# Gate projections of three branches by seven products of half size instead of eight

## The chip, the cores and the metric

The kernel runs on one core of a Trainium2 chip. The metric is the device time of one run in microseconds, the median of several. The engines named below are PE (matmuls, with its weight loads), DVE, ACT and POOL (elementwise), and SP, whose queue issues the DMAs.

## The reference

Two layers of a mixer. Each takes 1152 tokens (128 of a prompt, 1024 of a sample) of width 1024, modulates and normalises them to h, and projects h by one matrix w_in to the inputs of three branches and to a merge gate for each:

```
fx, fz, rq, rk, rv, rz, aq, ak, av, az, mg = split_columns(h @ w_in)
ya = (fourier_mix(fx) @ w_four) * silu(fz)
yb = rms_norm(retention(rq, rk, rv)) * silu(rz)
yc = windowed_attention(aq, ak, av) * silu(az)
ga, gb, gc = split(sigmoid(mg), 3)
merged = ga * (ya @ w_pa) + gb * (yb @ w_pb) + gc * (yc @ w_pc)
x = x + gate * rms_norm(merged @ w_out)
```

The gates mg are 3072 columns of w_in: the largest projection of a layer. The change concerns them, and the products with w_pa, w_pb and w_pc that they scale.

## The kernel before

h lies transposed in SBUF, features on the partitions, eight tiles of 128 features by 1152 tokens, split into a high and a low part (HH, HL) of fp32r. A weight tile is split in the same way: ACT casts the high part (L174), POOL subtracts (L175). A product of the two is three matmuls, high by high, high by low, low by high. A gate tile of 128 columns is loaded as one unit of 512 KB, `unit_t`; for each of three chunks of 384 tokens, `proj_t` (L214 to L221) runs 8 x 3 matmuls into a PSUM bank.

The layer runs in stages: the projection of retention's keys and values, constants of retention, the Fourier branch, retention over nine tiles of tokens (`ret_a` makes scores, L817 to L825; `ret_b` the output and its norm, L842 to L866), queries of attention, the gates az of attention, attention itself (nine tiles), and the output projection. `branch(br, ...)` (L904 to L959) computes for a branch: the rows of its y from DRAM; then per 128 output columns the gate tile, its tanh (L938), the branch product (L941 to L943), the scaling of one by the other (L944, DVE), the sum with the branch before (L956, POOL), a store to DRAM. Branches 0 and 1 stand behind attention in the program, branch 2 behind them with its result kept in SBUF.

The framework orders the instructions of each engine ahead of time by a simulated timeline, and every engine then runs its list in order. So the matmuls of branches 0 and 1, which need only h and y, are placed between those of retention's end and of attention. A list is fixed: an engine whose next instruction waits does nothing else. `tick()` (L481) steps the modulation of the next layer (L446, DVE) beside the projections.

The retention's result is stored by SP (L879) after its ninth tile. The DMAs of w_in's gate columns are issued by SP too (L188).

## Time and profile before

| | |
|---|---|
| median of 3 runs | 2015.68 us (2013.76 to 2015.83) |
| profiled execution | 2026.52 us, span 2024.7 us |
| PE | 1968.2 us, 97% |
| DVE | 1033.1 us, 51% |
| ACT | 676.1 us, 33% |
| POOL | 551.5 us, 27% |

The profiled execution is 0.5% slower than the median. The busy time of a matmul overlaps that of the next, so a mean duration on the page is a latency; what a matmul costs PE is the distance between two starts in the timeline. The stages of the first layer that the change touches are, by PE: the end of retention (396 to 455 us), attention (455 to 835), and the gates behind it (835 to 934); in the second layer 1390 to 1441, 1441 to 1792 and 1792 to 1920.

### The profile page before, as it was taken

Reading aid. Unit: us, or ns where it says so; the run is one execution under the profiler, and the core shown is the slowest. Engines: PE = TensorE matmul, PEld = TensorE weight load, DVE = VectorE, ACT = ScalarE, POOL = GpSimd, SP = SyncE. Lnnn points to the kernel's source line nnn. Section 1 sums busy time; section 2 is a strip of 40 time slices with the busy share of each in tenths; the row PEclk is TensorE's granted clock in tenths of the full one; section 3 lists DMA queues with packets and bytes.
Section 4 is the critical chain, followed back from the end, with each engine's and each line's share of the span. In section 5 each row is a group of like instructions: output and inputs, shape, how many; then the busy total and the mean of one; then the engine's idle time right before and its main releaser. Section 6 shows DMA issues by size and latency. Waiting matters only on the chain.

```text
span 2024.7 us, 30761 instructions
## 1 busy us (share of the span) xinstructions
PE 1968.2 (97%) x11334; PEld 1818.2 (90%) x11334; DVE 1033.1 (51%) x2675; ACT 676.1 (33%) x1563; POOL 551.5 (27%) x424
## 2 busy tenths in 40 slices
PE   5999999999999999999999999999999999999998
PEld 2898888999999999999877978799999999999987
DVE  6726556545677775414674262434356655531411
ACT  3522111214444555414331212022345554531411
POOL 2222232121122221254441203122121223234342
PEclk8999999999999999999999999999999999999999
DMA  8323553434343332333344134233333333342142
GB/s 293 100 71 100 155 148 117 129 117 137 112 123 114 114 102 65 116 118 128 118 142 96 58 94 146 82 118 95 124 107 102 108 101 97 93 132 90 55 146 93
DMA packets 245190, 230.58 MB, mean 114 GB/s; under 512 B 37920, under 2 KB 215856, under 8 KB 244784
## 3 DMA queue, kind: packets, MB, share of 16 engines
q1 hardware_dynamic: 245040, 228.62, 37.5%
q8 instruction: 89, 1.46, 0.3%
q14 instruction: 61, 0.50, 0.1%
HBM read 170.14 MB, written 58.42 MB: 113 GB/s over the span
## 4 chain that ended last, share of the span: by engine, by line
PE 88%; DVE 4%; DMA 4%; issue 1%; ACT 1%; SPq 1%; POOL 0%; DVEq 0%; POOLq 0%; ACTq 0%
PE pj L218 13%; PE pj L219 13%; PE pj L220 13%; PE pj L229 5%; PE pj L228 5%; PE pj L230 5%; PE pv L1099 4%; PE tr L1092 3%; PE sl L1038 2%; PE sl L941 2%; PE sl L943 2%; PE sl L942 2%; DMA raw<-in_w_in 2%; PE pj L941 2%; PE pj L942 2%; PE sl L230 2%
## 5 line engine op out<-in xcount | busy, mean ns | idle before, releaser
L218 PE MATMUL pj<-HH,uh 128*128 128x384 f32 x1440 | 496.0, 344 | 11.9 <-DVE XL L653 5.7
L220 PE MATMUL pj<-HH,ul 128*128 128x384 f32 x1440 | 491.5, 341 | 0.0
L219 PE MATMUL pj<-HL,uh 128*128 128x384 f32 x1440 | 489.6, 340 | 0.0
L175 POOL TENSOR_TENSOR ul<-raw,uh 128x1024 fp32r<-128x1024 f32 x80 | 193.6, 2421 | 513.9 <-ACT uh L174 420.4
L218 PEld LDWEIGHTS pj<-HH,uh 128*128 128x128 f32 x1440 | 273.5, 190 | 16.7 <-DVE XL L653 6.0
L219 PEld LDWEIGHTS pj<-HL,uh 128*128 128x128 f32 x1440 | 273.7, 190 | 0.7
L220 PEld LDWEIGHTS pj<-HH,ul 128*128 128x128 f32 x1440 | 273.3, 190 | 1.0
L174 ACT CAST uh<-raw 128x1024 fp32r<-128x1024 f32 x80 | 83.9, 1049 | 176.3 <-PE pj L219 108.2
L446 DVE SCALAR_TENSOR_TENSOR macc<-mw,siluc,macc 128x256 f32<-128x256 f32 x224 | 134.1, 639 | 8.4 <-DMA mw<-in_w_mod 8.4
L228 PE MATMUL pj<-uh,HH 128*128 128x512 f32 x336 | 134.1, 400 | 3.5 <-ACT kv L546 1.9
L229 PE MATMUL pj<-ul,HH 128*128 128x512 f32 x336 | 133.5, 397 | 0.0
L230 PE MATMUL pj<-uh,HL 128*128 128x512 f32 x336 | 132.9, 396 | 0.0
L1075 ACT ACTIVATE E<-E,NM 128x640 f32<-128x640 f32 (+1 forms) x128 | 101.8, 798 | 53.0 <-DVE NM L1071 52.9
L1095 ACT CAST Eh<-tr 128x512 fp32r<-128x512 f32 (+1 forms) x136 | 76.3, 574 | 113.9 <-PE tr L1092 101.0
L1096 DVE TENSOR_TENSOR El<-tr,Eh 128x512 fp32r<-128x512 f32 (+1 forms) x136 | 90.6, 671 | 36.3 <-ACT Eh L1095 29.7
L956 POOL TENSOR_TENSOR mth<-mth,ml 128x384 f32<-128x384 f32 x48 | 52.1, 1086 | 187.6 <-DVE mth L944 144.3
L944 DVE SCALAR_TENSOR_TENSOR M<-M,sl 128x384 f32<-128x384 f32 x48 | 26.5, 553 | 133.1 <-PE sl L943 132.6
L1056 DVE CUSTOM_DVE_ANT_0 E<-sl,mask,m 128x384 f32<-128x384 f32 (+1 forms) x128 | 71.9, 580 | 30.4 <-PE sl L1038 30.0
L1092 PE MATMUL tr<-ident,E 128*128 128x128 f32 x528 | 85.6, 273 | 0.0
L228 PEld LDWEIGHTS pj<-uh,HH 128*128 128x128 f32 x336 | 63.4, 189 | 18.4 <-ACT kv L546 2.1
L1052 DVE TENSOR_SCALAR_CACHE_REDUCE E<-sc 128x256 f32<-128x256 f32 x128 | 49.3, 421 | 60.1 <-PE sc L1038 59.4
L944 DVE SCALAR_TENSOR_TENSOR mth<-mth,pj 128x384 f32<-128x384 f32 x96 | 52.9, 551 | 52.4 <-ACT mth L938 27.8
(305 smaller groups left out, 4134.8 us busy)
## 6 DMA issues: line engine op xcount, KB each, us to landing
raw<-in_w_in SPq DMA_DIRECT2D x84, 512.0 KB, 4.0
scr_m<-mth SPq DMA_DIRECT2D x96, 192.0 KB, 2.4
mw<-in_w_mod SPq DMA_DIRECT2D x128, 128.0 KB, 2.5
scr_n<-ns SPq DMA_DIRECT2D x36, 256.0 KB, 2.4
ml<-scr_m SPq DMA_DIRECT2D x48, 192.0 KB, 2.5
mrow<-scr_m SPq DMA_DIRECT2D x16, 576.0 KB, 5.1
big<-in_w_mod SPq DMA_DIRECT2D x16, 512.0 KB, 4.8
raw<-in_w_out SPq DMA_DIRECT2D x16, 512.0 KB, 4.0
```

Of the source, the lines that this page charges most:

```text
L174: ACT.copy(hi, raw)
L175: POOL.tensor_tensor(out=lo, in0=raw, in1=f(hi), op=ALU.subtract)
L218: PE.matmul(acc, hi[:, k, :], HH[:, k, tok], start=(k == 0), stop=False)
L219: PE.matmul(acc, hi[:, k, :], HL[:, k, tok], start=False, stop=False)
L220: i = PE.matmul(acc, lo[:, k, :], HH[:, k, tok], start=False, stop=(k == KT - 1))
L228: PE.matmul(acc, a, hi[:, k % 2, :], start=(k == 0), stop=False)
L229: PE.matmul(acc, a, lo[:, k % 2, :], start=False, stop=False)
L230: i = PE.matmul(acc, b, hi[:, k % 2, :], start=False, stop=(k == KT - 1))
L446: DVE.scalar_tensor_tensor(out=accs[s], in0=w, scalar=siluc[:, k, s : s + 1], in1=accs[s], op0=ALU.mult, op1=ALU.add,)
L1075: ACT.activation(Es[hh][:, 0:nk], srcs[hh], AF.Exp, bias=NM[t][:, hs + hh : hs + hh + 1], scale=0.125, accum_out=DEN[t][:, hs + hh : hs + ...
L1092: PE.transpose(pt[:, i, hh, :], Es[hh][:, (n + i) * P : (n + i + 1) * P], ident)
L1096: DVE.tensor_tensor(out=El[:, :w], in0=pt, in1=f(Eh[:, :w]), op=ALU.subtract)
```

## The change

A gate pair is two column blocks (256 columns) by half of the tokens (576, in two halves of 288). Halves of the 1024 features, of the pair's columns and of the tokens make a 2 by 2 block product, which Strassen's scheme in Winograd's form computes by seven block products instead of eight. Each block product is 4 k-tiles x 3 matmuls of 288 columns (L953 to L960, `product`); a pair has 84. The sums of weights and of outputs are made in `gate_pair` (L964 to L1016): the weights' by DVE and POOL, on the raw tile, and each operand is then split by ACT and POOL; the outputs' by DVE. The sums of h, T1 to T4, depend on no gate column and are computed once a layer, after the first projection stage (L577 to L598); they and three blocks of h itself that are wanted again later go to DRAM, high and low part. `gates_half(s)` (L1036) loads them into the regions of HH and HL given by the table AT, when h itself is used no more, and runs all three branches for half s. The gates of branch 2 go to DRAM (gc_d); `merge` (L1074) reads them and branch 1's sum per tile of 128 columns. Attention's E buffers go from 6 to 4 and the weight pool wp is closed for the gates' stage.

```diff
 TOK = NT * P
 CH = 384
 NCH = 3
+SC = 576
+HN = 288
...
+        with pool("tp", side="right") as tp:
+            for s in range(2):
+                lt, rt = slice(s * SC, s * SC + HN), slice(s * SC + HN, (s + 1) * SC)
+                k1, k2 = slice(0, 4), slice(4, 8)
+                b = {}
+                for n, ks, tk in (("12", k1, rt), ("11", k1, lt), ("22", k2, rt), ("21", k2, lt)):
+                    b[n] = mk(tp, [P, 4, HN], "b" + n)
+                    POOL.tensor_tensor(out=b[n], in0=f(HH[:, ks, tk]), in1=f(HL[:, ks, tk]), op=ALU.add)
+                    if "B" + n in BLK[s]:
+                        for i, H in enumerate((HH, HL)):
+                            SP.dma_start(blk_dl[l][s]["B" + n][i].rearrange("p (a b) -> p a b", a=4), f(H[:, ks, tk]))
+                DVE.tensor_tensor(out=b["11"], in0=b["12"], in1=b["11"], op=ALU.subtract)
+                DVE.tensor_tensor(out=b["12"], in0=b["22"], in1=b["12"], op=ALU.subtract)
+                DVE.tensor_tensor(out=b["22"], in0=b["22"], in1=b["11"], op=ALU.subtract)
+                DVE.tensor_tensor(out=b["21"], in0=b["21"], in1=b["22"], op=ALU.subtract)
+                for n, t in (("T2", "22"), ("T3", "12"), ("T1", "11"), ("T4", "21")):
+                    th = mk(tp, [P, 4, HN], "th", F32R, bufs=2)
+                    tl = mk(tp, [P, 4, HN], "tl", F32R, bufs=2)
+                    ACT.copy(th, b[t])
+                    DVE.tensor_tensor(out=tl, in0=b[t], in1=f(th), op=ALU.subtract)
+                    for i, x in enumerate((th, tl)):
+                        SP.dma_start(blk_dl[l][s][n][i].rearrange("p (a b) -> p a b", a=4), f(x))
...
+        def block(s, n):
+            k0, t0 = AT[s][n]
+            return HH[:, k0 : k0 + 4, t0 : t0 + HN], HL[:, k0 : k0 + 4, t0 : t0 + HN]
+        def load_block(s, n):
+            for i, x in enumerate(block(s, n)):
+                SP.dma_start(f(x), blk_dl[l][s][n][i].rearrange("p (a b) -> p a b", a=4))
+        def operand(src, eng=POOL):
+            hi, lo = (mk(gp, [P, 4, P], t, F32R, bufs=5) for t in ("oh", "ol"))
+            ACT.copy(hi, src)
+            eng.tensor_tensor(out=lo, in0=src, in1=f(hi), op=ALU.subtract)
+            return hi, lo
+        def product(acc, op, s, n, start, stop):
+            hi, lo = op
+            bh, bl = block(s, n)
+            for k in range(4):
+                PE.matmul(acc, hi[:, k, :], bh[:, k, :], start=start and k == 0, stop=False, skip_group_check=True)
+                PE.matmul(acc, hi[:, k, :], bl[:, k, :], start=False, stop=False, skip_group_check=True)
+                i = PE.matmul(
+                    acc, lo[:, k, :], bh[:, k, :], start=False, stop=stop and k == 3, skip_group_check=True
+                )
+            anchor["pe"] = i.ins
+        def gate_pair(c0, s, eng):
+            w = []
+            for h in range(2):
+                raw = mk(gp, [P, 4, 256], "raw", bufs=2)
+                last_w[0] = SP.dma_start(
+                    raw, w_in[h * 512 : h * 512 + 512, c0 : c0 + 256].rearrange("(k p) f -> p k f", p=P)
+                ).ins
+                w.append(raw)
+            a11, a12, a21, a22 = w[0][:, :, 0:P], w[1][:, :, 0:P], w[0][:, :, P:256], w[1][:, :, P:256]
+            def comb(eng, x, y, op):
+                o = mk(gp, [P, 4, P], "sf", bufs=3)
+                eng.tensor_tensor(out=o, in0=x, in1=y, op=op)
+                return o
+            def add(o, x, y):
+                anchor["dve"] = DVE.tensor_tensor(out=o, in0=x, in1=y, op=ALU.add).ins
+            th = [mk(mA, [P, SC], "gt", bufs=3) for _ in range(2)]
+            lt, rt = slice(0, HN), slice(HN, SC)
+            def tanh(j, tk, src=None):
+                ACT.activation(th[j][:, tk], th[j][:, tk] if src is None else src, AF.Tanh, scale=0.5)
+                tick()
+            o1 = operand(a11, eng)
+            s1 = comb(POOL, a21, a22, ALU.add)
+            s2 = comb(DVE, s1, a11, ALU.subtract)
+            x1 = pj([P, HN])
+            product(x1, o1, s, "B11", True, False)
+            p1 = mk(mA, [P, HN], "p1")
+            ACT.copy(p1, x1)
+            x2 = pj([P, HN])
+            product(x2, operand(s2), s, "T2", True, True)
+            s4 = comb(DVE, a12, s2, ALU.subtract)
+            u2 = mk(mA, [P, HN], "u2", bufs=2)
+            add(u2, p1, x2)
+            product(x1, operand(a12, eng), s, "B21", False, True)
+            tanh(0, lt, x1)
+            x3 = pj([P, HN])
+            product(x3, operand(comb(POOL, a11, a21, ALU.subtract)), s, "T3", True, False)
+            u3 = mk(mA, [P, HN], "u3")
+            add(u3, u2, x3)
+            x4 = pj([P, HN])
+            product(x4, operand(s1), s, "T1", True, False)
+            add(th[1][:, rt], u3, x4)
+            tanh(1, rt)
+            product(x3, operand(a22, eng), s, "T4", False, True)
+            add(th[1][:, lt], u2, x3)
+            tanh(1, lt)
+            product(x4, operand(s4), s, "B22", False, True)
+            add(th[0][:, rt], u2, x4)
+            tanh(0, rt)
+            return th
+        def weights_of(pl, wb, nk, c0, n):
+            braw = mk(pl, [P, nk, n], "braw")
+            SP.dma_start(braw, wb[:, c0 : c0 + n].rearrange("(k p) f -> p k f", p=P))
+            bh = mk(pl, [P, nk, n], "bh", F32R, bufs=2)
+            bl = mk(pl, [P, nk, n], "bl", F32R, bufs=2)
+            ACT.copy(bh, braw)
+            POOL.tensor_tensor(out=bl, in0=braw, in1=f(bh), op=ALU.subtract)
+            return bh, bl
+        def mixed(pb, bh, bl, YH, YL, tok):
+            nk = len(YH)
             for kt in range(nk):
+                PE.matmul(pb, bh[:, kt, :], YH[kt][:, tok], start=(kt == 0), stop=False)
+                PE.matmul(pb, bh[:, kt, :], YL[kt][:, tok], start=False, stop=False)
+                PE.matmul(pb, bl[:, kt, :], YH[kt][:, tok], start=False, stop=(kt == nk - 1))
+        def gates_half(s):
+            t0 = s * SC
+            for n in ("T2", "T3", "T1", "T4") if s == 0 else ("B11", "T2", "B21", "T3", "T1", "T4"):
+                load_block(s, n)
+            if s == 0:
+                load_block(1, "B22")
+            for br in range(3):
+                if br < 2:
+                    YH, YL = [], []
+                    for kt in range(2):
+                        YH.append(mk(mA, [P, SC], f"yh{kt}", F32R))
+                        YL.append(mk(mA, [P, SC], f"yl{kt}", F32R))
+                        yr = mk(mA, [P, SC], "yr")
+                        SP.dma_start(yr, y_d[br * 256 + kt * P : br * 256 + (kt + 1) * P, t0 : t0 + SC])
+                        ACT.copy(YH[kt], yr)
+                        DVE.tensor_tensor(out=YL[kt], in0=yr, in1=f(YH[kt]), op=ALU.subtract)
+                for jp in range(4):
+                    th = gate_pair(C_MG + br * D + jp * 256, s, DVE if s and br == 2 else POOL)
+                    for jj in range(2):
+                        rows = slice(jp * 256 + jj * P, jp * 256 + (jj + 1) * P)
+                        if br < 2:
+                            wb = (ins["w_branch_a"], ins["w_branch_b"])[br][l]
+                            bh, bl = weights_of(mA, wb, 2, jp * 256 + jj * P, P)
+                            for q in range(2):
+                                tk = slice(q * HN, (q + 1) * HN)
+                                pb = pj([P, HN])
+                                mixed(pb, bh, bl, YH, YL, tk)
+                                anchor["dve"] = DVE.scalar_tensor_tensor(
+                                    out=th[jj][:, tk], in0=th[jj][:, tk], scalar=1.0, in1=pb, op0=ALU.add, op1=ALU.mult
+                                ).ins
+                        if br == 1:
+                            ml = mk(mA, [P, SC], "ml")
+                            SP.dma_start(ml, ma_d[0][rows, t0 : t0 + SC])
+                            POOL.tensor_tensor(out=th[jj], in0=th[jj], in1=ml, op=ALU.add)
+                        SP.dma_start((gc_d if br == 2 else ma_d[br])[rows, t0 : t0 + SC], th[jj])
+        def merge(pl, M):
+            YH, YL = ([H[:, 4 + kt, :] for kt in range(4)] for H in (HH, HL))
             for c in range(NCH):
                 tok = slice(c * CH, (c + 1) * CH)
+                for kt in range(4):
+                    n = c * 4 + kt
+                    yr = M[6 + n % 2][:, n // 2 % NCH * CH : n // 2 % NCH * CH + CH]
+                    SP.dma_start(yr, y_d[512 + kt * P : 512 + (kt + 1) * P, tok])
                     ACT.copy(YH[kt][:, tok], yr)
                     DVE.tensor_tensor(out=YL[kt][:, tok], in0=yr, in1=f(YH[kt][:, tok]), op=ALU.subtract)
             for j in range(KT):
+                bh, bl = weights_of(pl, ins["w_branch_c"][l], 4, j * P, P)
+                rows = slice(j * P, (j + 1) * P)
+                mrow = mk(pl, [P, TOK], "mrow", bufs=2)
+                SP.dma_start(mrow, ma_d[1][rows, :])
+                grow = mk(pl, [P, TOK], "grow", bufs=2)
+                SP.dma_start(grow, gc_d[rows, :])
                 for c in range(NCH):
                     tok = slice(c * CH, (c + 1) * CH)
+                    pb = (pj if c % 2 else sl)([P, CH])
+                    mixed(pb, bh, bl, YH, YL, tok)
+                    DVE.scalar_tensor_tensor(
+                        out=M[j][:, tok], in0=grow[:, tok], scalar=1.0, in1=pb, op0=ALU.add, op1=ALU.mult
+                    )
+                    POOL.tensor_tensor(out=M[j][:, tok], in0=M[j][:, tok], in1=mrow[:, tok], op=ALU.add)
...
-        branch(0, mA, mA, 0, None)
-        branch(1, mA, mA, 0, None)
+        for s in range(2):
+            gates_half(s)
         ma_st.close()
+        gst.close()
+        wst[0] = ExitStack()
+        wpc[0] = wst[0].enter_context(pool("wp"))
...
-        with pool("mg2", side="right") as m2, pool("mg3", side="right") as m3:
+        with pool("mg2", side="right") as m2:
             tick(1000)
-            branch(2, m2, m3, 0, M)
+            merge(m2, M)
 
```

On PE, at the end of retention in the first layer, before (tr, sl and pv are PSUM tiles of retention, L941 to L943 and L218 to L220 those of branch 0):

```order
L943 MATMUL pj_6213<-yh_1334_6010,bl_6183 128x384 [waits Pool_49]
L941 MATMUL pj_6213<-yh_1336_6012,bh_6182 128x384
L942 MATMUL pj_6213<-yl_1337_6013,bh_6182 128x384
L943 MATMUL pj_6213<-yh_1336_6012,bl_6183 128x384
L863 MATMUL tr_2613<-ident_67,o_2592 128x128 [waits DVE_49]
L863 MATMUL tr_2613<-ident_67,o_2592 128x128
L817 MATMUL tr_2621<-ident_67,kvq_2618 128x128 [waits DMAHW7_49]
L817 MATMUL tr_2621<-ident_67,kvq_2618 128x128 x3
L218 MATMUL pj_6228<-HH_77,uh_6176 128x384 [waits Activation_49]
L219 MATMUL pj_6228<-HL_78,uh_6176 128x384
L220 MATMUL pj_6228<-HH_77,ul_6177 128x384
```

and now, the last tile of retention, the first gate product at L957:

```order
L868 MATMUL pv_2749<-kvq_2700,A_2715 128x64 [waits DVE_49]
L868 MATMUL pv_2749<-kvq_2700,A_2715 128x64 x3
L897 MATMUL tr_2744<-ident_67,o_2723 128x128 [waits DVE_49]
L897 MATMUL tr_2744<-ident_67,o_2723 128x128
L897 MATMUL tr_2775<-ident_67,o_2754 128x128 [waits DVE_49]
L897 MATMUL tr_2775<-ident_67,o_2754 128x128
L957 MATMUL pj_6132<-HH_77,oh_6124 128x288 [waits Activation_49]
L958 MATMUL pj_6132<-HL_78,oh_6124 128x288
L959 MATMUL pj_6132<-HH_77,ol_6125 128x288 [waits Pool_49]
L957 MATMUL pj_6132<-HH_77,oh_6124 128x288
```

Before, gate products stand between two tiles of retention; now none stands before the last L897.

On SP at the same place, before (L879 is the store of retention's result, L188 a load of gate weights, L420 the modulation's weights):

```order
L420 DMA mw_6303<-in_w_mod 128x256 [waits DMAHW1_49,DVE_49]
L188 DMA raw_6848<-in_w_in 128x8x128 [waits DMAHW2_49,Pool_49]
L959 DMA scr_m_0<-mth_6293 128x384 [waits DMAHW3_49,DVE_49]
L420 DMA mw_6355<-in_w_mod 128x256 [waits DMAHW4_49,DVE_49]
L928 DMA braw_6585<-in_w_branch_a 128x2x128 [waits DMAHW5_49,Pool_49]
L959 DMA scr_m_0<-mth_6345 128x384 [waits DMAHW6_49,DVE_49]
L420 DMA mw_6395<-in_w_mod 128x256 [waits DMAHW7_49,DVE_49]
L879 DMA scr_y<-grz_1917 128x1152 [waits DMAHW0_49,DVE_49]
L879 DMA scr_y<-grz_1917 128x1152 [waits DMAHW1_49,DVE_49]
L922 DMA yr_7123<-scr_y 128x384 [waits DMAHW2_49,DMAHW0_49]
```

and now (L913 is that store, L969 the load of gate weights, L1022 of branch weights, L944 of a block of h):

```order
L944 DMA HL_78<-scr_b_1_B 128x4x288 [waits DMAHW3_49]
L1050 DMA yr_6108<-scr_y 128x576 [waits DMAHW4_49]
L1022 DMA braw_6283<-in_w_branch_a 128x2x128 [waits DMAHW5_49,Pool_49]
L1050 DMA yr_6114<-scr_y 128x576 [waits DMAHW6_49,DMAHW4_49,DVE_49]
L1022 DMA braw_6306<-in_w_branch_a 128x2x128 [waits DMAHW7_49,DMAHW5_49,Pool_49]
L1022 DMA braw_6488<-in_w_branch_a 128x2x128 [waits DMAHW7_49,DMAHW0_49,Pool_49]
L913 DMA scr_y<-grz_1999 128x1152 [waits DMAHW1_49,DVE_49]
L913 DMA scr_y<-grz_1999 128x1152 [waits DMAHW2_49,DVE_49]
L969 DMA raw_6118<-in_w_in 128x4x256 [waits DMAHW3_49]
L969 DMA raw_6120<-in_w_in 128x4x256
L430 DMA mw_6185<-in_w_mod 128x256
```

The loads of the gate weights have moved from in front of the store to behind it.

On DVE in the Fourier stage of the first layer, before (XL is the low part of the Fourier input, pj a projection's bank):

```order
L640 TENSOR_TENSOR MFl_885<-sl_890,MFh_884 128x512
L640 TENSOR_TENSOR MFl_885<-sl_895,MFh_884 128x512
L653 TENSOR_TENSOR XL_901<-pj_926,XH_900 128x384
L653 TENSOR_TENSOR XL_901<-pj_953,XH_900 128x384
L237 SCALAR_TENSOR_TENSOR gz_879<-gth_1005,pj_980 128x384
L444 TENSOR_SCALAR macc_192_1014<-mw_1008,siluc_73 128x256
L444 TENSOR_SCALAR macc_193_1015<-mw_1008,siluc_73 128x256
L237 SCALAR_TENSOR_TENSOR gz_879<-gth_1043,pj_1018 128x384
L446 SCALAR_TENSOR_TENSOR macc_192_1014<-mw_1010,siluc_73,macc_192_1014 128x256
```

and now (b and tl are the sums of h and their low parts):

```order
L652 SCALAR_TENSOR_TENSOR DD_947<-DD_947,rdf_907 128x512 [waits Activation_49]
L588 TENSOR_TENSOR b_159_856<-b_158_854,b_159_856 128x1152 [waits Pool_49]
L589 TENSOR_TENSOR b_158_854<-b_160_860,b_158_854 128x1152 [waits DVE_49]
L590 TENSOR_TENSOR b_160_860<-b_160_860,b_159_856 128x1152 [waits DVE_49]
L591 TENSOR_TENSOR b_161_864<-b_161_864,b_160_860 128x1152 [waits DVE_49,Pool_49]
L596 TENSOR_TENSOR tl_873<-b_160_860,th_872 128x1152 [waits DMAHW4_49,Activation_49]
L596 TENSOR_TENSOR tl_879<-b_158_854,th_878 128x1152 [waits DMAHW7_49,Activation_49]
L596 TENSOR_TENSOR tl_885<-b_159_856,th_884 128x1152 [waits DMAHW5_49,Activation_49]
L596 TENSOR_TENSOR tl_891<-b_161_864,th_890 128x1152 [waits DMAHW6_49,Activation_49]
L687 TENSOR_TENSOR XL_983<-pj_1008,XH_982 128x384 [waits DVE_49,Activation_49]
L687 TENSOR_TENSOR XL_983<-pj_1035,XH_982 128x384 [waits Activation_49]
```

The sums of h stand in front of the first XL.

## Rows read from the trace of the kernel before

**Rows 1.** The page: busy time of each engine; DMA rate in 40 slices.

```profile
PE 1968.2 (97%) x11334; PEld 1818.2 (90%) x11334; DVE 1033.1 (51%) x2675; ACT 676.1 (33%) x1563; POOL 551.5 (27%) x424
...
GB/s 293 100 71 100 155 148 117 129 117 137 112 123 114 114 102 65 116 118 128 118 142 96 58 94 146 82 118 95 124 107 102 108 101 97 93 132 90 55 146 93
```

**Rows 2.** Waits of PE, whole run: line, releaser, total, times, longest.

```profile
PE tr L308 <- DVE hrv L246: 7.8, 1, 7.8
```

**Rows 3.** Stretches: length, busy PE, PEld, DVE, ACT, POOL, clock, DMA share, GB/s.

```profile
396.10:455.10 59.00, 57.88 (x369) 54.63 (x367) 29.96 (x76) 13.90 (x28) 12.90 (x11) 1.00 0.39 123
455.10:834.70 379.60, 377.41 (x2446) 372.32 (x2447) 249.12 (x686) 182.46 (x434) 87.63 (x63) 1.00 0.36 104
834.70:934.00 99.30, 99.30 (x574) 99.30 (x573) 39.18 (x105) 34.88 (x107) 45.34 (x36) 1.00 0.39 123
1389.50:1440.70 51.20, 51.08 (x318) 47.99 (x316) 19.97 (x51) 12.04 (x26) 11.91 (x10) 1.00 0.36 117
1440.70:1791.60 350.90, 349.31 (x2290) 345.21 (x2290) 196.88 (x602) 175.58 (x426) 81.73 (x60) 1.00 0.33 98
```

**Rows 4.** Timeline of PE, gate products: start, duration, instruction.

```profile
1799.73 0.33 PE L220 MATMUL pj<-HH,ul 128*128 128x384 f32 x1
...
1800.77 0.34 PE L220 MATMUL pj<-HH,ul 128*128 128x384 f32 x1
```

**Rows 5.** Timeline of PE, products of 512 columns.

```profile
100.64 0.40 PE L229 MATMUL pj<-ul,HH 128*128 128x512 f32 x1
...
101.33 0.39 PE L229 MATMUL pj<-ul,HH 128*128 128x512 f32 x1
```

**Rows 6.** Source view of L863 between 320 and 460 us: one line.

```profile
L863 PE MATMUL tr<-ident,o x16: 271/272/273, 334.1 to 443.2; 128*128 128x128 f32 x16
```

**Rows 7.** Timeline of DVE, retention: the end of one tile; the next A.

```profile
384.69 0.74 DVE L848 TENSOR_TENSOR T<-sl,RD 128x256 f32<-128x256 f32 x2
...
389.59 0.42 DVE L860 TENSOR_TENSOR o<-o,orr 128x256 f32<-128x256 f32 x1 [0.90 <-POOL orr L248]
...
398.00 0.76 DVE L825 TENSOR_TENSOR A<-sl,DD 128x256 f32<-128x256 f32 x2
```

**Rows 8.** Timeline of ACT: the copy that starts a retention tile.

```profile
393.39 0.59 ACT L818 COPY qk<-tr 128x512 f32<-128x512 f32 x1 [2.12 <-PE tr L817]
```

**Rows 9.** Timeline of POOL, the same retention tile.

```profile
381.72 2.38 POOL L175 TENSOR_TENSOR ul<-raw,uh 128x1024 fp32r<-128x1024 f32 x1 [11.98 <-ACT uh L174]
388.45 1.11 POOL L248 TENSOR_TENSOR orr<-orv,mhalf 128x4 f32<-128x4 f32 x1 [4.36 <-DVE orv L246]
```

**Rows 10.** DMA issues: count, KB each, us to landing.

```profile
raw<-in_w_in SPq DMA_DIRECT2D x84, 512.0 KB, 4.0
```

**Rows 11.** POOL by form: count, busy us, mean ns, idle before.

```profile
L175 POOL TENSOR_TENSOR ul<-raw,uh 128x1024 fp32r<-128x1024 f32 x80 | 193.6, 2421 | 513.9 <-ACT uh L174 420.4 <-issue 36.2 <-PE pj L220 17.0
...
L932 POOL TENSOR_TENSOR bl<-braw,bh 128x256 fp32r<-128x256 f32 x32 | 25.2, 788 | 19.7 <-ACT bh L931 19.6
...
L932 POOL TENSOR_TENSOR bl<-braw,bh 128x512 fp32r<-128x512 f32 x16 | 21.1, 1316 | 22.2 <-ACT bh L931 22.2
```

**Rows 12.** Timeline of DVE in the Fourier stage: first XL.

```profile
112.16 0.56 DVE L653 TENSOR_TENSOR XL<-pj,XH 128x384 fp32r<-128x384 f32 x1 [1.84 <-ACT XH L652]
```

**Rows 13.** PE by line in the first layer's attention.

```profile
L218 PE MATMUL pj<-HH,uh 128*128 128x384 f32 x410 | 141.8, 346 | 2.0 <-ACT mth L938 1.7
...
L943 PE MATMUL pj<-yh,bl 128*128 128x384 f32 x78 | 26.8, 344 | 0.0
```

**Rows 14.** DVE by form in the first layer's attention.

```profile
L446 DVE SCALAR_TENSOR_TENSOR macc<-mw,siluc,macc 128x256 f32<-128x256 f32 x62 | 44.0, 745 | 0.1
...
L944 DVE SCALAR_TENSOR_TENSOR mth<-mth,pj 128x384 f32<-128x384 f32 x40 | 22.1, 551 | 21.5 <-ACT mth L938 11.5 <-PE pj L943 5.1 <-ACT Q L1012 3.6
```

**Rows 15.** Timeline of DVE, the same operation twice.

```profile
376.69 0.88 DVE L446 SCALAR_TENSOR_TENSOR macc<-mw,siluc,macc 128x256 f32<-128x256 f32 x2
...
382.53 2.24 DVE L446 SCALAR_TENSOR_TENSOR macc<-mw,siluc,macc 128x256 f32<-128x256 f32 x2
```

82 lines of the change are left out of this document (22 added, 60 removed).

## The prediction

> **What bounds the kernel now.** I read the page's busy line first. PE is busy for 1968.2 us, 97% of the span of 2024.7; DVE is at 51%, ACT at 33%, POOL at 27% [rows 1]. The waits of PE come next: the longest is 7.8 us, at the start [rows 2]. So the kernel is one in-order stream of matmuls, and two things move its time: how much PE work there is, and how much of the span PE stands idle. The windows by stage say where it is full today. From the end of the az projections to the start of attention in the first layer (396.10 to 455.10) it is busy for 57.88 of 59.00 us; in attention for 377.41 of 379.60; in the stretch behind it for all 99.30. The second layer reads the same: 51.08 of 51.20 and 349.31 of 350.90. The granted clock is 1.00 in all of them [rows 3]. In the first of these stretches retention's last tiles run, and the reader is to see that PE is full there only because branch 0's gate products stand between its small matmuls.
>
> **PE work taken away.** Six spacings of 384-column products take 1800.77 - 1799.73 = 1.04 us, 0.173 us each [rows 4]; the mean of one on the page is a latency and is not used. Three of 512 columns take 0.69 us, 0.230 each [rows 5]. Between them a column costs 0.44 ns, so 288 columns are estimated at 0.173 - 96 x 0.00044 = 0.131 us. Per layer the gates were 24 tiles x 3 chunks x 24 = 1728 products; now they are 3 branches x 4 pairs x 2 halves x 84 = 2016. So 1728 x 0.173 = 299 us becomes 2016 x 0.131 = 264. The branch products of branches 0 and 1 go from 288 x 0.173 = 50 to 384 x 0.131 = 50. That is 35 us less per layer, **70 us** in both: the upper bound of the gain. The saving is small, 7 products for 8, and less because a narrow product costs more per column.
>
> **Retention's tail: the filler goes.** The first product of the new gates cannot start before retention has ended. In the order of PE no gate product stands before the last L897; in the order of SP the load of the first weights (L969) stands behind the store of retention's result (L913), which waits for the last tile. The store is an issue that waits for DVE, and everything behind it on SP waits too: the weights, mod's loads, attention's mask and keys. So PE runs the last tiles alone. Before, 16 transposes L863 (8 tiles) lie between 334.1 and 443.2, some 15 us a tile with the filler [rows 6]; four of these tiles end behind 396.1. Without filler a tile takes its own chain. From T (384.69) to the normalised o (389.59 + 0.42) it is 5.3 us, and the masking of A is 0.76 [rows 7]; the copy of qk is 0.59 [rows 8]; POOL's power, 1.11, is in the 5.3 [rows 9]. With the transposes, scores and products of PE between them (some 1.5 us) a round is 5.7 to 9 us; I take 8. In the first layer three rounds stand behind the az gates, then the last two normalisations, 24 + 2, then the store and 4.0 us for 512 KB of weights [rows 10], a cast and the first difference: 34 us, of which PE works some 9. Idle: 25 us. In the second layer two to three rounds: 21. Sum **+46**, bounds 30 (rounds of 5.7) and 62.
>
> **The differences of h (T-stage).** Eight sums of 1152 columns go to POOL per layer, eight subtractions and eight differences to DVE. POOL takes 788, 1316 and 2421 ns for 256, 512 and 1024 columns [rows 11], 2.07 ns a column, so 1152 are estimated at 2.7 us. In the first layer POOL's order is weights, b22, weights, b12, b11, b21; the first weights come at 104 as in before, so the last sum ends near 106.5 + 2.7 + 2.4 + 3 x 2.7 = 119.7. DVE has the four subtractions and the four tl in front of the first XL (L687), each 1.2 to 1.8 us, the last ones beside nothing else: XL comes near 127. It was at 112.16 [rows 12], and the Fourier matmuls and the bank behind it wait for it: +15 us. In the second layer only the last sum is late: +5. Sum **+20**, bounds 5 and 35. The stores run beside projections and cost nothing.
>
> **The second half's blocks.** Between the halves of tokens six blocks of two parts, 12 x 590 KB = 7.1 MB, are loaded into the regions that the last pair has just read. At the fastest rate of any slice, 293 GB/s [rows 1], that is 24 us; a pair in attention takes about 20, and each block becomes free only when its last reader is through. **+5** per layer, bounds 0 and 15.
>
> **Attention.** The first layer's holds 1229 gate products and 234 branch products [rows 13], 1463 x 0.173 = 253; the rest of PE is 377 - 253 = 124. In the new order it holds 16 pairs, 1359 + 297 products x 0.131 = 217: PE 341, against 377. What stands beside them grows: DVE loses 40 operations L944 of 0.551 [rows 14] but gets per pair two sums of 512 (0.69 each, estimated from 0.48 for 256), five sums of 288 with a PSUM input (0.45) and four scalings (0.46) in eleven to twelve pairs, +59 and -1, on 249. That is 308. POOL goes from 87.63 [rows 3] to about 241: seven differences of 512 per pair at 1.316, two sums, the branch weights, some 15 us a pair. POOL's 71% is what counts, because DVE waits for it: two L446, both inputs in SBUF, take 0.88 us while POOL is idle and 2.24 beside the L175 of 381.72 [rows 15, 9]. The mean of L446 in attention is 745 ns where POOL is busy for 23% of it; at 71% such an operation would wait 0.47 us more (71% of half of 1.32). 62 L446, 32 new sums and some 60 smaller ones wait, 150 x 0.47 = 70, less 17 already in the 745: DVE about 361. I take the stage at 365, 24 over PE's 341. In the second layer there is no mod work of that size: DVE about 264 + 50, under PE's 338, and I take +8. Sum **+32**, bounds 5 (no such waits) and 90 (both engines add up).
>
> This wait is what a page of the Trainium skill states: SBUF — State Buffer, section "SBUF: two separate sides", has DVE and GpSimd share one port pair by an exclusive lock, so that a DVE operation with two SBUF inputs fully blocks while a GpSimd operation holds it. The two rows of L446 agree, 2.24 against 0.88 us. By that rule the price of POOL's new work falls on DVE, and the change is dearer than either engine's sum says.
>
> **The gates behind attention.** Eight pairs are left. Four of branch 1 want from POOL 7 x 1.32 + 2 x 1.3 + 2 x 0.79 + 2 x 1.45 = 16.3 us, and from PE 108 x 0.131 = 14.1: POOL is the longer by 2.2, and with DVE's waits some 3. Four of branch 2 have three differences on DVE and are PE's, with a product waiting now and then for its operand. +8 per layer and +2 for the merge, whose 1.2 MB a tile now come by DMA. Sum **+20**, bounds 5 and 40.
>
> **Sum.** -70 + 46 + 20 + 10 + 32 + 20 = +58 us, bounds -25 and +187. The profiled execution took 2026.5 us, 0.5% over the median of 2015.7; a difference of this size carries over, so 2015.7 + 58 = 2074.
>
> **Rivals.**
> A, faster: the 70 us show, because PE stays the bound. Each addition must be at its lower end (30 + 5 + 0 + 5 + 5 = 45): -25, 1991 us. For it speaks PE's 97% and that DVE, ACT and POOL are at half or less over the span. Against it: the tail is a chain that nothing fills, and PE has no spare stage to catch up in.
> B, POOL becomes the bound through DVE: with such waits at their full length DVE in both layers' attention runs to 390 and 360 (an operation with two SBUF inputs waits out most of a POOL operation), and the four branch-1 pairs at 19 us. That is attention +71 and the gates +40, so -70 + 46 + 20 + 10 + 71 + 40 = +117: 2133 us. For it speak the rows of L446; against it, that half of DVE's operations read PSUM.
> C, the stalls are structural only: tail, T-stage and blocks as above, no wait by POOL: -70 + 46 + 20 + 10 + 5 + 5 = +16: 2032 us.
> That the change does not do what it says: the 84 products a pair stand in the order, so this gets no chance.
>
> **Chances.** The forecast's own case (2050 to 2105) 0.52; B (over 2105) 0.16; C (2020 to 2050) 0.12; A 0.15, and 0.05 for no difference. A measurement of this kernel can tell 0.2%, 4 us, from no change; so slower 0.80, same 0.05, faster 0.15. The range leaves out the better part of A and of B: 1998 to 2125. The likeliest case's own range is 2050 to 2105.
>
> **What would show it.** In the profile after: 288-column products 0.131 us apart; PE idle by 20 to 30 us between the last az product and the first L957, releasers DVE, POOL and the DMA of raw; a wait for XL of some 15 us near 112 to 127; POOL over 900 us in all; L446 in attention near 1 us; attention's PE busy 341 of 365. Wrong would be: the tail under 15 us, attention within 5 us of PE's work, or 288 columns nearer to 0.115 or 0.147 us (2400 products a layer: 38 us a layer either way).

## The result, and the profile after

| | before | after |
|---|---|---|
| median | 2015.76 us (4 runs, 2013.76 to 2018.9) | 2258.21 us (4 runs, 2250.37 to 2264.96) |
| ratio | | 1.120, interval 1.116 to 1.124 |
| PE | 97% | 88% |
| DVE | 51% | 61% |
| POOL | 27% | 47% |

The change makes the kernel 242 us slower. The forecast was 58 slower, 2074, and its range ended at 2125. The sign was right; the size was missed by a factor of four. The pages here are of the execution of 2264.96 us (before: 2026.52).

The page after, its span, busy line, PE's slices and the granted clock, answering [rows 1]:

```profile
span 2263.2 us, 34479 instructions
...
PE 1994.7 (88%) x12102; PEld 1805.6 (80%) x12102; DVE 1388.5 (61%) x3091; ACT 867.2 (38%) x1987; POOL 1062.8 (47%) x816
...
PE   6949999868898999879997699998799999988898
...
PEclk8979999969999999999998799998899999999899
```

PE is busy for 1994.7 us, longer than before, with less work. Behind the first slice, every slice below 8 is new, and in five of these six the granted clock falls too. The waits of PE after (line, releaser, total us, times, longest), answering [rows 2]:

```profile
PE pj L228 <- DVE XL L687: 38.4, 2, 29.5
PE pj L957 <- ACT oh L949: 21.9, 6, 8.5
PE sl L1032 <- ACT HH L1082: 15.6, 2, 8.0
PE tr L897 <- DVE o L894: 13.7, 8, 2.9
PE pj L238 <- ACT ns L558: 13.3, 2, 8.7
```

And the stretches (length; busy time of PE, PEld, DVE, ACT, POOL; clock; DMA share; GB/s), answering [rows 3]: the Fourier stage, retention's tail, attention and the gates behind it in the first layer, then the last three in the second.

```profile
113.90:301.30 187.40, 147.44 (x749) 132.81 (x747) 106.40 (x186) 37.25 (x64) 52.84 (x36) 0.90 0.42 134
437.60:486.60 49.00, 23.55 (x116) 18.99 (x116) 20.22 (x52) 7.33 (x16) 8.51 (x8) 0.55 0.59 199
486.60:877.80 391.20, 355.50 (x2590) 338.82 (x2589) 334.66 (x816) 234.52 (x565) 234.02 (x186) 0.98 0.47 143
877.80:1010.00 132.20, 114.68 (x789) 108.83 (x787) 58.21 (x97) 54.50 (x113) 94.35 (x74) 0.96 0.50 156
1560.40:1603.10 42.70, 19.58 (x95) 15.56 (x94) 16.84 (x45) 6.68 (x15) 8.50 (x8) 0.56 0.63 214
1603.10:1964.00 360.90, 342.67 (x2561) 332.33 (x2560) 265.35 (x715) 233.45 (x565) 230.65 (x185) 0.99 0.45 140
1964.00:2100.00 136.00, 115.44 (x795) 109.00 (x793) 57.87 (x98) 55.50 (x114) 96.63 (x75) 0.97 0.50 158
```

The reader is to see that no stage is full any more. Laid out by PE's first instruction of each stage, the first layer's Fourier stage took 146.6 us (107.1 to 253.7) and takes 187.4; with the projection ahead of it, it is 48 us later at its end. In the second layer the time from the layer's start to this end is 34 longer. From the last az product to the end of the layer the first layer took 575.6 us (396.1 to 971.7) and takes 673.4 (437.6 to 1111.0); the second 635.2 and 702.8. These four differences make 248, and retention's own stages are 9 shorter: 239 of the 238.5 us between the spans.

In the Fourier stage, DVE after, answering [rows 12]: five differences HL with the sums beside them, a low part of the sums, a product of eight columns, another low part with its wait for a store, and the first XL.

```profile
86.20 13.05 DVE L400 TENSOR_TENSOR HL<-big,HH 128x384 fp32r<-128x384 f32 x5
...
114.46 1.34 DVE L596 TENSOR_TENSOR tl<-b,th 128x1152 fp32r<-128x1152 f32 x1
115.73 2.63 DVE L622 TENSOR_TENSOR lz<-ls 128x8 f32<-128x8 f32 x1
...
149.83 1.36 DVE L596 TENSOR_TENSOR tl<-b,th 128x1152 fp32r<-128x1152 f32 x1 [3.05 <-DMA scr_b_T<-tl]
...
152.92 1.01 DVE L687 TENSOR_TENSOR XL<-pj,XH 128x384 fp32r<-128x384 f32 x2
```

POOL in the same stretch: four sums of the first half, a low part of weights (L185), and the first and the last two sums of the second half:

```profile
87.15 11.68 POOL L584 TENSOR_TENSOR b<-HH,HL 128x1152 f32<-128x1152 f32 x4
111.66 2.86 POOL L185 TENSOR_TENSOR ul<-raw,uh 128x1024 fp32r<-128x1024 f32 x1 [12.82 <-ACT uh L184]
114.47 3.86 POOL L584 TENSOR_TENSOR b<-HH,HL 128x1152 f32<-128x1152 f32 x1
...
126.33 2.61 POOL L584 TENSOR_TENSOR b<-HH,HL 128x1152 f32<-128x1152 f32 x1 [2.78 <-DVE lq L626]
130.31 2.61 POOL L584 TENSOR_TENSOR b<-HH,HL 128x1152 f32<-128x1152 f32 x1 [1.37 <-DVE lg L630]
```

The product of eight columns (L622) ends at 118.36, with the sum of POOL beside it (118.33). XL comes at 152.92; it came at 112.16. In the tail, PE's timeline (in brackets the idle time ahead and its releaser):

```profile
456.09 1.97 PE L868 MATMUL pv<-kvq,A 128*128 128x64 f32 x8 [4.74 <-DVE o L887]
...
482.70 0.61 PE L957 MATMUL pj<-HH,oh 128*128 128x288 f32 x1 [8.11 <-ACT oh L949]
...
485.17 0.45 PE L957 MATMUL pj<-HH,oh 128*128 128x288 f32 x1
485.41 0.45 PE L958 MATMUL pj<-HL,oh 128*128 128x288 f32 x1
```

and SP:

```profile
475.01 0.81 SPq L913 DMA_DIRECT2D scr_y<-grz  x2
475.87 2.29 SPq L969 DMA_DIRECT2D raw<-in_w_in  x2
```

PE runs the last tiles alone and waits 8.11 us for the first weights, whose load stands behind the store, as the order said. Of the 45.1 us from the last az product (437.6) to the first gate product PE is busy for 20.15. The first products are 0.24 us apart (485.17 to 485.41); in the gates behind attention, six spacings take 0.80 us:

```profile
905.21 0.29 PE L958 MATMUL pj<-HL,oh 128*128 128x288 f32 x1
...
906.01 0.29 PE L958 MATMUL pj<-HL,oh 128*128 128x288 f32 x1
```

That is 0.133 us for 288 columns at a granted clock of 1.00. The 0.24 us behind the idle tail are at a granted clock of 0.50, the lower of its two levels, 1.2 GHz.

In the first layer's attention, DVE and POOL by form, answering [rows 14] and [rows 11]:

```profile
L456 DVE SCALAR_TENSOR_TENSOR macc<-mw,siluc,macc 128x256 f32<-128x256 f32 x74 | 56.8, 799 | 0.1
...
L977 DVE TENSOR_TENSOR sf<-sf,raw 128x512 f32<-128x512 f32 x16 | 17.7, 1108 | 10.3 <-POOL sf L977 10.3
```

```profile
L950 POOL TENSOR_TENSOR ol<-sf,oh 128x512 fp32r<-128x512 f32 x65 | 87.9, 1359 | 56.2 <-ACT oh L949 50.1 <-PE pj L959 3.6 <-DVE sf L977 1.3
```

### The profile page after: what moved, and what is told of

It is laid out like the page before. It is cut to its first block, busy times and chain, and to the rows that moved or that the text cites. A ratio compares the mean times of both kernels' runs of the same rounds, so it can differ in the third digit from the quotient of the medians.

```text
span 2263.2 us, 34479 instructions
## 1 busy us (share of the span) xinstructions
PE 1994.7 (88%) x12102; PEld 1805.6 (80%) x12102; DVE 1388.5 (61%) x3091; ACT 867.2 (38%) x1987; POOL 1062.8 (47%) x816
## 5 line engine op out<-in xcount | busy, mean ns | idle before, releaser
L957 PE MATMUL pj<-HH,oh 128*128 128x288 f32 x1344 | 414.1, 308 | 51.2 <-ACT oh L949 21.9
L959 PE MATMUL pj<-HH,ol 128*128 128x288 f32 x1344 | 405.7, 303 | 9.5 <-POOL ol L950 7.8
L958 PE MATMUL pj<-HL,oh 128*128 128x288 f32 x1344 | 403.0, 300 | 0.0
L950 POOL TENSOR_TENSOR ol<-sf,oh 128x512 fp32r<-128x512 f32 x192 | 258.9, 1358 | 127.0 <-ACT oh L949 104.4
L957 PEld LDWEIGHTS pj<-HH,oh 128*128 128x128 f32 x1344 | 258.5, 192 | 64.2 <-ACT oh L949 24.6
L959 PEld LDWEIGHTS pj<-HH,ol 128*128 128x128 f32 x1344 | 257.8, 192 | 13.8 <-POOL ol L950 11.6
L958 PEld LDWEIGHTS pj<-HL,oh 128*128 128x128 f32 x1344 | 258.5, 192 | 0.0
L950 POOL TENSOR_TENSOR ol<-raw,oh 128x512 fp32r<-128x512 f32 x120 | 160.5, 1337 | 61.4 <-ACT oh L949 58.1
L456 DVE SCALAR_TENSOR_TENSOR macc<-mw,siluc,macc 128x256 f32<-128x256 f32 x224 | 152.3, 715 | 8.6 <-DMA mw<-in_w_mod 8.4
L185 POOL TENSOR_TENSOR ul<-raw,uh 128x1024 fp32r<-128x1024 f32 x32 | 79.4, 2485 | 147.7 <-ACT uh L184 147.5
L228 PE MATMUL pj<-HH,uh 128*128 128x384 f32 x288 | 100.7, 350 | 7.0 <-ACT ns L558 3.2
L228 PE MATMUL pj<-HH,xh 128*128 128x384 f32 x192 | 68.8, 358 | 38.4 <-DVE XL L687 38.4
L230 PE MATMUL pj<-HH,ul 128*128 128x384 f32 x288 | 99.9, 347 | 0.0
L1238 DVE TENSOR_TENSOR El<-tr,Eh 128x512 fp32r<-128x512 f32 (+1 forms) x136 | 90.0, 669 | 15.9 <-ACT Eh L1237 14.7
```

The source lines that it names most:

```text
L228: PE.matmul(acc, hi[:, k, :], HH[:, k, tok], start=(k == 0), stop=False)
L230: i = PE.matmul(acc, lo[:, k, :], HH[:, k, tok], start=False, stop=(k == KT - 1))
L456: DVE.scalar_tensor_tensor(out=accs[s], in0=w, scalar=siluc[:, k, s : s + 1], in1=accs[s], op0=ALU.mult, op1=ALU.add,)
L950: eng.tensor_tensor(out=lo, in0=src, in1=f(hi), op=ALU.subtract)
L957: PE.matmul(acc, hi[:, k, :], bh[:, k, :], start=start and k == 0, stop=False, skip_group_check=True)
L958: PE.matmul(acc, hi[:, k, :], bl[:, k, :], start=False, stop=False, skip_group_check=True)
```

## The experiments

All times are medians beside runs of the kernel before on the same chip (2014 to 2019 us). What a kernel leaves out stands in its expectation. The interval of a kernel's ratio is 0.003 to 0.007 to either side, 6 to 14 us, so that a difference of two kernels is known to some 10 us.

**The sums alone in the kernel before.** Added at the changed kernel's place:

```diff
+        with pool("tp", side="right") as tp:
+            for s in range(2):
+                ...
         rc_st = ExitStack()
```

> The kernel before with the stage of sums added (L577 to L598 of the changed kernel: eight sums on POOL, sixteen operations of 1152 columns on DVE, eight casts, the stores), which nothing reads. Theory: POOL's sums and DVE hold each other up, and the first XL comes near 150 us instead of 112; with the second layer this is 55 to 75 us, so 2070 to 2090 us. Rival (the prediction's size): 20 us, 2036. Second rival: the delay of XL comes from the changed kernel's other pools and not from the sums: no change, 2016.

Measured: 2109.9 us, ratio 1.046 (1.042 to 1.050): 91 to 94 us, more than either theory. Its waits of PE:

```profile
PE pj L226 <- DVE XL L685: 37.9, 2, 29.5
PE pj L236 <- ACT ns L556: 17.0, 2, 10.9
```

The two waits for XL are those of the changed kernel to half a microsecond (37.9, 38.4). The stage costs this by itself, whatever the gates are.

**The sums left out of the change, their DMAs kept.**

```diff
-                    POOL.tensor_tensor(out=b[n], in0=f(HH[:, ks, tk]), in1=f(HL[:, ks, tk]), op=ALU.add)
-                ... the subtractions, casts and differences
...
+                        SP.dma_start(blk_dl[l][s][n][i].rearrange("p (a b) -> p a b", a=4), f(H[:, ks, tk]))
```

> The changed kernel with the sums left out: the blocks are stored straight from HH and HL by the same number and size of DMAs, so POOL, DVE and ACT do nothing for them; the products then use unsummed blocks. Theory: the sums' engine work is what costs, 55 to 75 us less, 2185 to 2205 us. Rival: the stores (20 MB over both layers, beside the loads of weights) hold up the Fourier stage: at most 15 us less, 2243 or more.

Measured: 2164.28 us, 94 less than the changed kernel. So it is the engines' work, and not the bytes that the stores move (26 MB by the kernel, 20 in the expectation). One wait for the stores goes with the work: the low parts tl have two buffers, and DVE stands still for 3.05 us in the profile after (149.83) until a store has freed one. This run has no tl and does not price that wait.

**One low part for all weight operands.**

```diff
...
-            eng.tensor_tensor(out=lo, in0=src, in1=f(hi), op=ALU.subtract)
+            if not lo_c:
+                lo_c.append(mk(gp, [P, 4, P], "ol", F32R))
+                eng.tensor_tensor(out=lo_c[0], in0=src, in1=f(hi), op=ALU.subtract)
+            lo = lo_c[0]
```

> The changed kernel with the low part of a weight operand computed once a layer and used for all products: POOL loses 334 differences of 512 columns at 1.35 us, 450 us of its 1063, DVE a few; matmuls, casts, sums and output sums stay. Theory: POOL, and DVE's waits for it, hold attention (391 and 361 us against 337 and 333 of matmuls) and the gates behind it (132 and 136 against 104): attention falls by 30 and 18, the gates by 20 each, 2258 - 88 = 2170 us. Rival: it is DVE's own work and the chain product, output sum, tanh in two banks; then at most 30 us less, 2228 or more, with DVE's means of two-input operations falling all the same.

Measured: 2127.18 us, ratio 1.055 (1.048 to 1.062), 131 less; more than expected. Two things changed: its pool is 8 KB smaller too, and its first gate products stood at 438.7, inside the tail. The run with four buffers of ol, below, has the tail filled and the low parts kept, and the difference of the two is the low parts alone. (Of the 334 low parts 312 are POOL's, 419 us; the others are DVE's.) DVE in its first attention:

```profile
L456 DVE SCALAR_TENSOR_TENSOR macc<-mw,siluc,macc 128x256 f32<-128x256 f32 x56 | 27.9, 537 | 0.0
...
L982 DVE TENSOR_TENSOR sf<-sf,raw 128x512 f32<-128x512 f32 x16 | 11.0, 689 | 15.0 <-POOL sf L982 14.9
```

L456 is at 537 ns where it was at 799, the sum at 689 where it was at 1108.

**Filler for the tail, by order.**

```diff
+AZ_AT = (0, 0, 1, 1, 2, 3, 3, 4, 5, 5, 6, 7)
...
-                    proj_t(u, c, acc)
+                    with tc.issue_after(ret_pe[AZ_AT[i * NCH + c]]):
+                        proj_t(u, c, acc)
```

> The changed kernel with the az projections, 12 groups of 24 matmuls a layer, tied behind retention's tiles 0 to 7 one after the other, so that the last tiles have matmuls between them; nothing else is changed. Theory: the idle time of the tail (437.6 to 482.7 and 1560.4 to 1599.2, some 27 and 25 us without work) is the lack of filler, and most of it goes: 30 to 45 us less, 2213 to 2228, with 8 us left for the first weights behind retention's store. Rival: the chain of a tile is as long as before and the stall only moves to the earlier tiles, which lose the filler: 0 to 10 us less, 2248 to 2258.

Measured: 2284.3 us, 26 slower than the changed kernel. Both theories fall. The tail's waits shrank, but the last az product, now at 476, is also the last reader of h, so the blocks' loads came only then, and the first weights stood behind them on SP. The last wait of PE and the loads in question:

```profile
PE pj L963 <- ACT oh L955: 19.4, 1, 19.4
```

```profile
474.82 1.25 SPq L950 DMA_DIRECT2D HH<-scr_b_T  x2
...
487.04 1.95 SPq L975 DMA_DIRECT2D raw<-in_w_in  x2
```

**Both costs out.** The two edits of the sums' DMAs and of the one low part together.

> The changed kernel with both costs out: blocks stored unsummed as in the run that had the sums' DMAs only (94 us less), and one low part of a weight operand a layer (131 us less; its pool is 8 KB smaller, and its gates filled retention's tail too). Theory: the two costs add, 2258 - 94 - 131 = 2033 us. Rival: they are the same wait seen twice (POOL full in both stages, and what is left is bound by PE): then less than the sum, 2070 or more. If it comes under 1990, PE's saving shows and nothing else of the change costs.

Measured: 2028.83 us, ratio 1.009 (1.002 to 1.016). The costs add: 2033 was expected. And even here, with neither sums nor low parts nor an empty tail, the kernel is not faster. Its page:

```profile
span 2026.2 us, 33803 instructions
...
PE 1919.4 (95%) x12102; PEld 1759.3 (87%) x12102; DVE 1205.4 (59%) x3035; ACT 851.0 (42%) x1971; POOL 588.5 (29%) x490
```

PE is busy for 49 us less than in the kernel before, and without work for 107 us where it was 57: the saving is there and is lost as idle time. What PE still waits for:

```profile
PE sl L1025 <- ACT HH L1075: 15.9, 2, 8.0
...
PE pj L950 <- DVE gt L974: 6.5, 9, 1.3
...
PE pj L950 <- DVE u L974: 6.0, 4, 2.6
PE pj L1025 <- ACT yh L1044: 5.6, 2, 3.9
```

**The sums later.**

```diff
-        with pool("tp", side="right") as tp:
+        with pool("tp") as tp:
+            for s in range(2):
+                for k in range(4):
+                    sums(tp, s, k)
         azp = mix.enter_context(pool("azp", side="right"))
```

> The changed kernel with the sums moved behind the Fourier stage, in eight pieces of one k-tile and 288 columns in a pool of 11 KB, ahead of retention's states; the same operations and bytes in smaller pieces (four times the instructions, about 0.3 us of start each on DVE and POOL). Theory: what the 94 us were is the place, in front of XL and among DVE's small operations; behind it PE has the projections of retention's gates and queries, and 55 to 75 us of it come back, 2185 to 2205 us. Rival: POOL's 28 us of sums now stand in front of retention's states (vw) and hold them up by as much: 0 to 30 us back, 2228 to 2258.

Measured: 2262.5 us: nothing gained. The rival named the right stage and the wrong instruction; PE waits for the scaling of retention's gate and not for its states:

```profile
PE pj L228 <- DVE grz L247: 110.0, 2, 55.7
```

In DVE's list the eight pieces stand ahead of that scaling (L247), which frees PE's bank. They follow one another from 243.6 to 291.5 us; in each, POOL's sums wait for DVE's low parts of the piece before, and DVE for a store of tl. (A start of 0.3 us an instruction, as the expectation has it, is too much for DVE: 0.46 us for 288 columns and 1.36 for 1152 leave some 0.16.) PE waits for the whole list, up to 55.7 us a layer.

**The low parts on DVE.**

```diff
-        def operand(src, eng=POOL):
+        def operand(src, eng=DVE):
...
-                    th = gate_pair(C_MG + br * D + jp * 256, s, DVE if s and br == 2 else POOL)
+                    th = gate_pair(C_MG + br * D + jp * 256, s, DVE)
```

> The changed kernel with all seven low parts of a pair on DVE instead of POOL (in branch 2 of the second half three already are). Theory: POOL's long operations block those of DVE that read two inputs in SBUF; without them the means fall back (L456 from 0.80 to 0.48 us, L1213 from 0.44 to 0.15, L977 from 1.0 to 0.7), about 56 us in the first layer's attention, against 114 x 0.69 = 79 us of new work; attention about as long as now (391 and 361: 375 to 395 and 345), gates behind it 8 us a layer shorter: 2215 to 2250 us. Rival: POOL's length is what holds, and DVE takes it at half the time: 60 us less, 2195. Other rival: DVE is the bound already, 60 us more.

Measured: 2220.4 us, 38 less, inside the theory's range. Its page, and its first attention:

```profile
PE 1980.8 (89%) x12102; PEld 1792.9 (81%) x12102; DVE 1506.8 (68%) x3403; ACT 868.8 (39%) x1987; POOL 655.8 (30%) x504
```

```profile
L950 DVE TENSOR_TENSOR ol<-sf,oh 128x512 fp32r<-128x512 f32 x71 | 48.8, 693 | 1.1 <-ACT oh L949 0.7
...
L456 DVE SCALAR_TENSOR_TENSOR macc<-mw,siluc,macc 128x256 f32<-128x256 f32 x74 | 36.8, 528 | 0.1
```

A difference takes DVE 693 ns and POOL 1359, and L456 is back at 528. DVE has 312 differences more, which at 693 ns are 216 us, and its busy time grows by 118 only (1388.5 to 1506.8): its other operations are shorter by the rest.

**A pool that fits.**

```diff
-            hi, lo = (mk(gp, [P, 4, P], t, F32R, bufs=5) for t in ("oh", "ol"))
+            hi, lo = (mk(gp, [P, 4, P], t, F32R, bufs=n) for t, n in (("oh", 5), ("ol", 4)))
```

> The changed kernel with four buffers of ol instead of five. The pool gp (34 KB) takes the place of wp (32 KB), and its last 2 KB lie on retention's constants (RD and rgn), which are read until the last tile; with four buffers it fits, and in the new order 200 gate products stand between retention's last tiles. Theory: these 2 KB are why the tail is empty, and with the filler its idle and slow time (37 and 31 us) goes down to some 10 a layer: 45 us less, 2213 us. Rival: with POOL's and DVE's gate work beside them retention's chains get longer by what is gained, or the operand queue of four buffers stalls PE: 0 to 15 us less.

Measured: 2216.48 us, ratio 1.101 (1.096 to 1.105), 42 less, as the theory has it. The two tails, a stretch of 53 and of 50 us:

```profile
437.00:490.00 53.00, 41.38 (x292) 36.90 (x291) 37.07 (x76) 17.04 (x36) 29.16 (x24) 0.94 0.56 185
1560.00:1610.00 50.00, 45.27 (x299) 42.09 (x300) 29.99 (x68) 20.61 (x52) 33.12 (x29) 0.88 0.49 155
```

PE works for 41.4 and 45.3 us there, at a clock of 0.94 and 0.88; in the changed kernel for 23.55 of 49 and 19.58 of 42.7, at 0.55 and 0.56. Two kilobytes kept the tail empty.

**The sums on DVE, in their place.**

```diff
-                    POOL.tensor_tensor(out=b[n], in0=f(HH[:, ks, tk]), in1=f(HL[:, ks, tk]), op=ALU.add)
+                    DVE.tensor_tensor(out=b[n], in0=f(HH[:, ks, tk]), in1=f(HL[:, ks, tk]), op=ALU.add)
```

> The changed kernel with the eight sums HH + HL of a layer on DVE instead of POOL; place and everything else unchanged. Theory: the sums' 94 us are mostly DVE standing still beside POOL's sums of 2.7 us (its own operations of 8 columns take 2.4 to 2.6 us each there, the five L400 13 us instead of 3.3); without them DVE has 24 operations at 1.36 = 33 us a layer, of which about half lies in slack: XL near 130 to 137 instead of 153, and 35 to 50 us less over both layers, 2208 to 2223 us. Rival: it is the order on DVE alone (sums in front of XL, whoever computes them), and eight more operations there make it worse: 2258 or more.

Measured: 2227.71 us, 30 less, a little short of the range. The same instructions of DVE as shown for the changed kernel:

```profile
84.71 3.27 DVE L400 TENSOR_TENSOR HL<-big,HH 128x384 fp32r<-128x384 f32 x5
...
110.75 0.15 DVE L622 TENSOR_TENSOR lz<-ls 128x8 f32<-128x8 f32 x1
...
138.92 1.01 DVE L687 TENSOR_TENSOR XL<-pj,XH 128x384 fp32r<-128x384 f32 x2
```

The five L400 take 3.27 us for 13.05, the product of eight columns beside the sum (L622) 0.15 for 2.63, and XL comes at 138.9, 14 us earlier. So about a third of the sums' 94 us goes when POOL does not make them. With XL earlier PE's two waits for it are not shorter (46.4 us in all, 38.4 in the changed kernel), since PE comes to them earlier too. That the other two thirds are the place in front of XL is likely and not shown: DVE has 24 operations of some 1.35 us there in each layer, and the run with the sums later put them in front of another instruction.

**Fit and low parts together; and the sums as well.**

> The changed kernel with four buffers of ol (the pool fits and the tail has filler: 42 us less) and all low parts on DVE (38 us less). Theory: separate causes in separate places, the gains add: 2178 us. Rival: with filler in the tail, gate work starts earlier and DVE is the next bound in the first layer's attention: 2195 or more.

> The kernel of the run before (four buffers of ol, low parts on DVE) with the sums on DVE as well. Theory: adds again, 2135 to 2145 us, and still well over the kernel before, since DVE now carries what POOL did. Rival: 2160 or more, the sums' gain being lost to the same DVE.

Measured: 2186.86 us, ratio 1.085 (1.081 to 1.088), and 2165.25, 1.074 (1.070 to 1.078). The first lies between theory and rival: by medians 42 + 38 would be 80 and it is 71, by the ratios beside the kernel before 74 and 72, so within the noise the two gains add. The second lies in the rival's range. The sums give 22 more where they gave 30 alone; no run tells these two apart, and that DVE, with the work of POOL on it, takes the difference is not shown. The last is the best complete version found, and it is 7% slower than the kernel before.

**No reloading of blocks.** The run with both costs out, without its loads:

```diff
-            for n in ("T2", "T3", "T1", "T4") if s == 0 else ("B11", "T2", "B21", "T3", "T1", "T4"):
-                load_block(s, n)
-            if s == 0:
-                load_block(1, "B22")
```

> The kernel with both costs out (2029 us, 1.009 of before), and the blocks not loaded back: the products read h where it stands, 24 loads of 590 KB a layer are gone; stores stay. It asks what eats PE's 61 us there. Theory: the reloads at the change from h to blocks, between the halves, and before the merge's y: 10 to 25 us less, 2004 to 2019, ratio 0.995 to 1.004. Rival: the waits of each product for its sums, tanh and banks, and the merge's wait for y (8 us a layer): 0 to 8 us less, ratio over 1.005.

Measured: ratio 1.0054 (1.0038 to 1.0071), against 1.0094 (1.0024 to 1.0163) with the loads. The intervals overlap; the reloads (22 a layer, by the kernel) cost 8 us at the most likely, and between none and some 25. The ratio is in the rival's range, but its interval reaches into the theory's, so the two are not told apart.

## Why the prediction was wrong

Two terms of the sum failed by their size: the sums of h, at +20, cost 94, and attention with the gates and the merge, at +52, cost some 157. By edits the 242 us are made of four parts, each known to some 10 us: the sums 94 (added and taken away), the empty tail 42, the low parts some 90 (1.101 with a filled tail against 1.055 with one and no low parts), and 15 that are left when all three are out. In these 15 PE's saving is included.

- **PE's work, -70.** The estimate of 0.131 us for 288 columns was 0.133: per layer 2400 x 0.133 = 319 for 349 before, a saving of 59 us over both, not 70. Right in kind, 11 off. That it is taken away shows in PE's busy time of the run with both costs out, 49 us less.
- **Retention's tail, +46.** Measured as 42 by the kernel whose pool fits. The mechanism (no filler, weights behind the store) was as read, and PE's idle time in it was as forecast, 25 us in the first layer and 23 in the second for 25 and 21. The chain was longer than my 34 us, 45 from the last az product (437.6) to the first gate product (482.7): part of it ran at the lower clock, and one tile was held by 4.74 us, by DVE. That the emptiness came from 2 KB of a pool lying on retention's constants I had not seen; I took the order as given. The run with az as filler shows that order alone is no cure, since az reads what the blocks' loads overwrite.
- **The sums, +20, bounds 5 and 35: the step that failed first.** It had POOL's sums end near 119.7 and XL near 127; the last sum ended at 132.9 and XL came at 152.9. Four things were left out. Operations of DVE with two SBUF inputs, even of eight columns, wait out a POOL operation of 2.6 us beside them. I had this from the rows of L446 [rows 15] and used it for attention only, where I looked for it. The weights' first low part (L185), taken at 104 as before, started at 111.66, behind ACT's cast. The last two sums of the second half wait, 2.78 and 1.37 us, until DVE has read their buffers, so that POOL and DVE run in turns there. And the stores, forecast at nothing, hold DVE's last low parts back (3.05 us ahead of the one at 149.83). In the second layer I took 5 us by the place of one sum; it was 34 by stage. Some 74 us of the miss are here; what each of the four is worth was not measured apart, but for the third that goes with POOL's sums.
- **Blocks, +10.** 0 to 25 by the last run, likeliest 8: not contradicted.
- **Attention and the gates behind it, +32 and +20: mis-sized.** Attention's PE work is 1603 products x 0.133 + 124 = 337 in the first layer, and it took 391; in the second 1598 x 0.133 + 120 = 332, and it took 361. That is 54 and 29 over, for my 24 and 8. DVE's 334.66 lie below my 361 and POOL's 234 near my 241. The busy sums were not too low, and the rule that I made of them, that the stage ends with its longest engine (365), failed. PE is idle for 36 us in the first attention, in waits of at most 2.5 us, most of them for DVE (the sums of products, the scalings), and only 0.6 for a low part of POOL. An operand passes ACT, POOL, PE, DVE and ACT in turn, each in a fixed order; that at 86% of DVE and 60% of POOL the waits add up over this chain is my reading, which no run isolates. The gates behind it: 132 and 136 us for 787 and 792 products at 0.133 = 105; I had 8 over, it is 27 and 31. The low parts, taken out, are worth some 90 in these places.
- **The merge, +4.** PE waits some 8 us a layer for attention's y, which is loaded and copied into h's place as the last blocks are read (the wait for HH L1082); 16 in all. With attention and the gates this makes 54 + 29 + 27 + 31 + 16 = 157 for 52. The misses, 74 + 105 + 11 less 4 for the tail and 2 for the blocks, add up to the 184 us between forecast and result.

The rivals: A, PE's saving shows, had its test in the run with both costs out, and did not come in the time even there. C, stalls of structure alone, falls with the low parts. B, the POOL-and-DVE rival at +117, was the nearest, in its mechanism too. The page SBUF — State Buffer of the Trainium skill, section "SBUF: two separate sides", says that a DVE operation with two SBUF inputs blocks in full while a POOL operation holds the shared ports. The traces agree: L456 took 0.80 us with POOL's low parts, 0.54 and 0.53 without, and a product of eight columns 2.63 beside a sum and 0.15 without one. Its error was to price the wait in attention and not wherever POOL had been idle.

What stays open is the rest of the run with both costs out: PE has 59 us less to do there and the kernel is 15 us slower, so some 74 us are lost, 50 of them as more idle time of PE in the profile. The wait for y (15.9), for yh (5.6) and for sums and tanh of a pair (6.5, 6.0 and smaller ones) are read from its list of waits; no run took them away one by one.

## What to carry to other kernels

A product scheme that saves an eighth of the matmuls paid nothing here, because its sums and splits lay on engines that had no time to spare at their place; price such work with the waits between DVE and POOL in every stage that POOL enters anew, not only in the one under study. When a stage that was full falls idle, look for the memory as well as the order: a new pool 2 KB larger than the one whose place it takes emptied a stage here. And busy sums of several engines in a chain are a lower bound of a stage, not its length.
